# Hybrid S5 / HGRN2 block: three jobs side by side at the start, and S5 from step 12

## The chip, the cores and the metric

One core of a Trainium2 chip runs the whole program in one launch. The metric is the device time of one execution in microseconds (us), a median over runs; the profile is of one further execution. Engines in the profile: PE is TensorE (matmul), PEld its weight loads, DVE VectorE, ACT ScalarE, POOL GpSimd; SP issues most of the DMAs.

## The reference, cut to what matters

```python
h    = rmsnorm(x, ln_mix_g)                      # x: 256 tokens x 2048
proj = h @ w_in                                  # 2048 x 9216
u, q, f, i, g, gate_s5, gate_hgrn = split(proj)  # 5 x 1024, 2 x 2048
y_s5   = s5_branch(u) @ w_proj_s5                # complex scan, gelu, GLU with w_glu
y_hgrn = hgrn2_branch(q, f, i, g) @ w_proj_hgrn  # gated recurrence, chunked
merged = sigmoid(gate_s5) * y_s5 + sigmoid(gate_hgrn) * y_hgrn
x = x + merged @ w_out
x = x + conv_glu_ffn(rmsnorm(x, ln_ffn_g))       # w_up 2048 x 11264, w_down
out = rmsnorm(x, ln_final_g)
```

All in float32; the matmuls are made of split operands (below).

## The kernel before

**Steps and jobs.** Every large matrix is read once, in 480 steps of 512 KB. A step loads a piece of weights (load_step, line 247, tile wr, 4 buffers, queue of SP), splits it (split_step, line 252: ACT copies it into a rounded high part wh, then DVE subtracts for the low part wl, 3 buffers each) and multiplies it: 8 matmuls of wh with 512 columns (the high and low halves of the activations side by side) and 8 of wl with 256, or in the jobs written token by token 8 and 4 of 512. A job is some steps that add into one PSUM bank pair (tile mm, two of them) and an epilogue (`st.after`) that DVE and ACT run on the sum one step later. The jobs in order: 4 of u and 4 of q (4 steps each, steps 0 to 31), 2 of g (16 steps), 4 of f (16), 4 and 4 of the gates (64), 2 of v (16, up to step 143); then GLU (steps 144 to 151), w_proj_s5 (152 to 167), w_proj_hgrn (168 to 183), w_out, w_up and w_down.

**The start.** x is loaded in four chunks of 512 columns. x_chunk (line 393) transposes a chunk on PE in 8 transposes; ACT writes the high part of hT with the gain of the norm (line 405) and DVE the low part. x_first (line 419) does chunk 0 and the split of step 0, with 6 warm-up matmuls behind it (tile dummy, on ones); chunks 1 to 3 are put between the two halves of steps 0, 1 and 2 (`between`), so that a job takes one chunk per step. The 1/rms of the rows is not needed for the products: x_norm (line 427) squares x on DVE in 8 instructions, issued behind step 2, and broadcasts the result R_x with PE; epilogues multiply by it. x_params transposes packed parameters.

**The side work and its planner.** Two generators hold the work that is not of the weight steps: side_s5 (line 580; tables, then 8 tiles in two pairs each: projection b_proj on PE, two products on DVE, a scan on DVE, two products, an output on PE) and side_hgrn (line 874: loads of q, k, f, scores on PE and masks and products on DVE over 7 levels, then o, its norm, its transposes). side_run (line 1303) is called after each step from S5_START = 3 on and emits pieces of them while an account allows it: all instructions of DVE and PE are charged an estimate (lines 76 to 92), and a piece is emitted when DVE's sum isn't above PE's:

```python
rate = {"tensor_copy": 0.52, "tensor_scalar": 0.52, "reciprocal": 6.3}.get(name, 1.04)
return 0.065 + 1.12e-3 * rate * n
...
if force in done if force is not None else load["dve"] > load["pe"] + SIDE_LEAD:
    return
```

At most 2 (S5) or 3 (HGRN) pieces a step are emitted. HGRN comes when S5 is finished. Two due dates are hard: step 144 needs all of S5, and step 168 all of HGRN (`need`). What isn't emitted by then is emitted at once, in front of that step: `if st.need not in done: side_run(force=st.need)` (line 1350), whatever the account says.

**What orders the instructions.** The framework's scheduler takes the program's order as priorities: an engine's instructions are put into a fixed queue, and one of lower priority can be put ahead where the scheduler finds the engine free and its inputs and buffers ready. behind_x (line 414) forbids that for what is emitted within it: it stays behind the last chunk of x.

Of the kernel before, what the change touches and what calls it, by code (L numbers as in the profile page):

```python
# [10 lines left out]
F32 = mybir.dt.float32  # L11
F32R = mybir.dt.float32r
# [5 lines left out]
P = 128  # L18
D = 2048
T = 256  # L20
# [90 lines left out]
def kernel(  # L111
# [48 lines left out]
    def axbank():  # L160
        uid[0] += 1
        return psx.tile([P, 512], F32, tag="ax", name=f"ax{uid[0]}")

    def v3(t, n):
        return t.rearrange("p (a b) -> p a b", a=n)
# [8 lines left out]
            return self.units[k // 4][:, (k % 4) * T:(k % 4 + n) * T]  # L174


    ones = cst.tile([P, P], F32, name="ones")
    G.memset(ones, 1.0)
# [7 lines left out]
    S.dma_start(out=cf, in_=cst_f)  # L186
    ident = cf[:, C_ID:C_ID + P]

    x_tok = [[unit() for _ in range(2)] for _ in range(2)]
    pack = unit()  # L190
    packA, packB = pack[0:104, 0:P], pack[0:64, P:2 * P]
    packC = [pack[0:P if i < 2 else 96, (2 + i) * P:(3 + i) * P] for i in range(3)]
# [1 line left out]
    def rows(ap):  # L194
        return ap.rearrange("o (r c) -> (o r) c", c=P)

    packG = pack[0:16, 6 * P:7 * P]
    S.dma_start(out=packG, in_=rows(ln_mix_g))
    G.memset(packA, 0.0)
    ldt = pack[0:64, 5 * P:5 * P + 2]  # L200

# [38 lines left out]
    def weight_step(src, mm, need=None, extra_load=None):  # L240
        st = Step()
        st.src, st.mm, st.need, st.extra_load = src, mm, need, extra_load
        st.after = st.between = None
        steps.append(st)
        return st

    def load_step(st):
        uid[0] += 1
        st.w = wp.tile([P, 1024], F32, tag="wr", name=f"wr{uid[0]}", bufs=4)
        S.dma_start(out=v3(st.w, st.src.shape[1]), in_=st.src)  # L250

    def split_step(st):
        uid[0] += 1
# [17 lines left out]
    def fm_job(wap, c0, nkc, xs, epi, need=None, extra_load=None, wide=False):  # L271


        job = new_job()
        box = {}
        ng = nkc // 4
        for g in range(ng):
            def mm(st, g=g):
                if g == 0:
                    box["ps"] = mm_bank()  # L280
                ps = box["ps"]
                wh, wl = v3(st.wh, 4), v3(st.wl, 4)
                for part in range(2):
                    if part == 1 and st.between is not None:
                        st.between()
# [107 lines left out]
    def x_chunk(g, between=None):  # L393

        for h in range(2):
            if h == 1 and between is not None:
                between()
            ax = axbank()
            for a in range(2):
                for j in range(2):  # L400
                    c = (g % 2) * 512 + (2 * h + a) * P
                    lastp = PE.transpose(ax[:, a * T + j * P:a * T + (j + 1) * P], x_tok[j][g // 2][:, c:c + P], ident)
            for a in range(2):
                kc = 4 * g + 2 * h + a
                A.activation(out=hT[:, kc, 0, :], in_=ax[:, a * T:(a + 1) * T], func=AF.Copy, scale=g_mix[:, kc:kc + 1])  # L405
# [5 lines left out]
        box["x"] = [getattr(i, "ins", i) for i in (last, lastp)]  # L411

    @contextmanager
    def behind_x():

        with tc.issue_after(box["x"][0]), tc.issue_after(box["x"][1]):
            yield

    def x_first():
        ax = axbank()  # L420
        PE.transpose(ax[:, 0:16], packG, ident[:16, :16])
        V.tensor_copy(g_mix, ax[:, 0:16])
        x_chunk(0, lambda: split_step(steps[0]))
        with behind_x():
            warm_up(WARM_H, ones)

    def x_norm():
        ss = cst.tile([P, 2, 4], F32, name="ss_x")
        for g in range(4):
            for j in range(2):  # L430
                xc = x_tok[j][g // 2][:, (g % 2) * 512:(g % 2) * 512 + 512]
                junk = tmp()
                V.scalar_tensor_tensor(out=junk, in0=xc, scalar=1.0, in1=xc, op0=ALU.mult, op1=ALU.mult,
                                       accum_out=ss[:, j, g:g + 1])
# [3 lines left out]
        broadcast_rows(R_x, r_x)  # L438

    def x_params():  # L440
        ax = axbank()
# [89 lines left out]
    u_jobs = [fm_job(w_in, 256 * p, 16, xs_hw, epi_u(p), wide=True) for p in range(4)]  # L531
    for p in range(4):
        fm_job(w_in, 1024 + 256 * p, 16, xs_hw, epi_q(p), wide=True)
    for b in range(2):
# [339 lines left out]
    def side_hgrn():  # L874
        yield f_job
        mraw = reload_tile()
        S.dma_start(out=mraw[:, 0:112], in_=cst_m)
        V.tensor_copy(masks, v3(mraw[:, 0:80], 5))
        q, k, f = (Chunks(8) for _ in range(3))
        for p in range(4):  # L880
            for t, src in ((q, q_dram), (k, k_dram), (f, f_dram)):
# [443 lines left out]
                if pauses[0] >= PAUSES[side[0]]:  # L1325
                    return

    for i in range(LOAD_AHEAD):
        if i < 4:
            load_x_chunk(i)  # L1330
        load_step(steps[i])
        if i == 4:
            load_params()
    table_up()
    warm_up(WARM, ones)
    x_first()
    for i in range(1, LA):
        split_step(steps[i])
    for i in range(3):
        steps[i].between = lambda i=i: x_chunk(i + 1)  # L1340
    load["dve"] = load["pe"] = 0.0
    for i, st in enumerate(steps):
        if i + LOAD_AHEAD < len(steps):
            load_step(steps[i + LOAD_AHEAD])
        if i + LA < len(steps):
            split_step(steps[i + LA])
# [11 lines left out]
        if i == NORM_AT:  # L1358
            with behind_x():
                x_norm()  # L1360
                x_params()
        if st.after is not None:
            job, fn = st.after
            later.append((i + 1, job, fn))
        load["dve"] = max(load["dve"], load["pe"] - 4.0)
        if i >= S5_START:
            pauses[0] = 0
            if i == S5_START:
                with behind_x():
                    side_run()  # L1370
            else:
                side_run()
    run_later(i=len(steps) + 10)


# [28 lines left out]
```

## Time and profile before

| | |
|---|---|
| median of 3 runs | 1423.0 us (1422.8 to 1423.98) |
| the profiled execution | 1422.75 us, span 1420.6 us |
| PE busy | 1403.4 us (99% of the span) |
| DVE busy | 1056.9 us (74%) |
| ACT busy | 757.7 us (53%) |
| DMA | 278.58 MB, mean 196 GB/s |

A row of a timeline is: start, length (us), engine, line, operation, out<-in, shape, how many were merged, and in brackets how long the engine sat idle before it and what released it. The line is often 106, that of the helper which keeps the account; so tiles tell the work apart: mm is a weight step, ax a transpose or a small product, bu a projection of S5, u any of the large work tiles. A row of the chain of waits is start, length, what. A row of windows is the stretch, its length, then the busy time and count of PE, PEld, DVE, ACT and POOL, the granted clock of PE, the DMA share and GB/s.

### The profile page before, as it was taken

How to read it: one execution, taken by the hardware profiler on the slowest of the kernel's cores; microseconds unless marked ns; L12 is line 12 of the kernel's file. 1: busy time of each engine (PE TensorE's matmuls, PEld its weight loads, DVE VectorE, ACT ScalarE, POOL GpSimd, SP SyncE). 2: the span in 40 equal slices, each digit the busy share in tenths (PEclk: the TensorE clock that was granted, in tenths of full speed). 3: DMA queues.
4: the chain of work that ended last, by engine and by line, in shares of the span. 5: the costliest groups of instructions: out<-in, count | busy, mean ns of one | idle time of the engine just before them, and what ended most of it. 6: DMA issues, size and time to landing. Idle time of an engine off the chain costs nothing.

```text
span 1420.6 us, 20722 instructions
## 1 busy us (share of the span) xinstructions
PE 1403.4 (99%) x8008; PEld 1182.1 (83%) x8008; DVE 1056.9 (74%) x1453; ACT 757.7 (53%) x962; POOL 38.0 (3%) x33
## 2 busy tenths in 40 slices
PE   9999999999999999999999999999999999999997
PEld 7878887877778787888888888888888888888885
DVE  7999989998978968655777777777777775545454
ACT  5455576665655464454555555555555554434343
POOL 1040000000001000000000000000000000000000
PEclk9999999999999999999999999999999999999999
DMA  7865767666767466666666666666666666666653
GB/s 237 219 195 149 218 206 219 202 205 187 210 191 262 154 199 207 220 212 207 193 191 185 188 192 187 186 191 191 185 189 191 188 187 193 201 193 201 194 194 125
DMA packets 215940, 278.58 MB, mean 196 GB/s; under 512 B 19938, under 2 KB 141042, under 8 KB 215841
## 3 DMA queue, kind: packets, MB, share of 16 engines
q1 hardware_dynamic: 198496, 266.57, 60.5%
q10 hardware_dynamic: 17088, 10.49, 2.4%
q8 instruction: 63, 1.03, 0.3%
q14 instruction: 37, 0.30, 0.1%
q0 software_dynamic: 256, 0.19, 0.0%
HBM read 266.73 MB, written 10.49 MB: 195 GB/s over the span
## 4 chain that ended last, share of the span: by engine, by line
PE 95%; DVE 2%; DMA 1%; ACT 1%; issue 0%; POOL 0%; ACTq 0%; DVEq 0%; POOLq 0%
PE mm L106 87%; PE ax L106 7%; DVE u L106 1%; PE bu L106 1%; DMA u<-d 1%; DVE wl L106 1%; DMA u<-in_s_log_dt_dram 0%; ACT wh L256 0%; DVE t L106 0%; PE dummy L106 0%; DVE zmat L106 0%; ACT u L1275 0%; DVE x2g L106 0%; ACT hT L405 0%; ACT t L1259 0%
## 5 line engine op out<-in xcount | busy, mean ns | idle before, releaser
L256 ACT CAST wh<-wr 128x1024 fp32r<-128x1024 f32 x480 | 503.0, 1051 | 587.7 <-PE mm L106 424.2
L106 DVE TENSOR_TENSOR wl<-wr,wh 128x1024 fp32r<-128x1024 f32 x480 | 588.2, 1228 | 304.3 <-ACT wh L256 301.3
L106 PE MATMUL mm<-x2g,wh 128*128 128x512 f32 x1408 | 352.6, 392 | 0.0
L106 PEld LDWEIGHTS mm<-x2g,wh 128*128 128x128 f32 x1408 | 253.3, 189 | 45.3
L106 PE MATMUL mm<-wh,u 128*128 128x512 f32 x1040 | 260.7, 392 | 0.0
L106 PEld LDWEIGHTS mm<-wh,u 128*128 128x128 f32 x1040 | 193.7, 188 | 39.7
L106 PEld LDWEIGHTS mm<-x2g,wl 128*128 128x128 f32 x1408 | 192.0, 190 | 13.6
L106 PE MATMUL mm<-x2g,wl 128*128 128x256 f32 x1408 | 196.4, 282 | 0.0
L106 PE MATMUL mm<-wh,hT 128*128 128x512 f32 x768 | 193.6, 394 | 0.0
L106 PEld LDWEIGHTS mm<-wh,hT 128*128 128x128 f32 x768 | 142.1, 188 | 33.5 <-issue 2.9
L106 PE MATMUL mm<-wl,u 128*128 128x512 f32 x520 | 140.6, 390 | 0.0
L106 DVE TENSOR_TENSOR u<-u,u 128x512 f32<-128x512 f32 (+4 forms) x144 | 114.8, 821 | 0.5
L106 PEld LDWEIGHTS mm<-wl,u 128*128 128x128 f32 x520 | 97.4, 188 | 20.0
L106 PE MATMUL mm<-wl,hT 128*128 128x512 f32 x384 | 102.9, 390 | 0.0
L106 PE MATMUL mm<-hT,wh 128*128 128x512 f32 x384 | 100.4, 401 | 0.8 <-ACT wh L256 0.8
L106 PEld LDWEIGHTS mm<-wl,hT 128*128 128x128 f32 x384 | 72.1, 188 | 15.5
L106 PEld LDWEIGHTS mm<-hT,wh 128*128 128x128 f32 x384 | 69.9, 192 | 14.8 <-ACT wh L256 1.0
L106 DVE SCALAR_TENSOR_TENSOR t<-ub,colC,t 128x256 f32<-128x256 f32 x176 | 73.3, 479 | 0.0
L106 PEld LDWEIGHTS mm<-hT,wl 128*128 128x128 f32 x384 | 52.1, 191 | 4.7 <-DVE wl L106 1.3
L106 PE MATMUL mm<-hT,wl 128*128 128x256 f32 x384 | 54.3, 284 | 0.3 <-DVE wl L106 0.3
L1200 ACT ACTIVATE t<-ub,colC 128x256 f32<-128x256 f32 x88 | 48.0, 593 | 0.0
L106 PE MATMUL ax<-wh,u 128*128 128x512 f32 x176 | 43.3, 389 | 0.0
(186 smaller groups left out, 861.2 us busy)
## 6 DMA issues: line engine op xcount, KB each, us to landing
wr<-in_w_up_dram SPq DMA_DIRECT2D x176, 512.0 KB, 4.5
wr<-in_w_in_dram SPq DMA_DIRECT2D x144, 512.0 KB, 4.4
wr<-in_w_down_dram SPq DMA_DIRECT2D x88, 512.0 KB, 4.7
wr<-in_w_out_dram SPq DMA_DIRECT2D x32, 512.0 KB, 4.2
wr<-in_w_proj_s_dram SPq DMA_DIRECT2D x16, 512.0 KB, 4.0
wr<-in_w_proj_hgrn_dram SPq DMA_DIRECT2D x16, 512.0 KB, 4.8
d<-t ACTq DMA_DIRECT2D x28, 256.0 KB, 4.4
rl<-d SPq DMA_DIRECT2D x16, 256.0 KB, 4.3
```

The source lines that it names most:

```text
L106: return fn(*args, **kw)
L256: A.copy(st.wh, st.w)
L1200: A.activation(out=av, in_=ub[:, a, 0:T], func=AF.Identity, scale=conv_col(0, n), bias=colC[:, 264 + n:265 + n])
```

## The change

The first three jobs (12 steps) no longer run one after the other: their steps are taken chunk by chunk of x (`FRONT = 3`: step g of jobs 0, 1, 2, then step g + 1 of them), so that a chunk serves three steps. The third job has its own PSUM pair (front_bank). In these 12 steps the order on SP, PE, ACT and DVE is the one written (manual_schedule). The first chunk of x and the first weight tile come in halves, the weights and the constants from ACT's queue, and the first step (`fine`) multiplies half by half, 24 matmuls of 256 columns instead of 16. A split runs one step ahead there and not two; 3 warm-up matmuls for 6. The squares of x go to ACT, chunk by chunk. The planner's account is set to zero at step 12, and side_run is called from step 12 on.

```diff
-    WARM_H = 6
-    NORM_AT = 2
+    WARM_H = 3
+    FRONT = 3
...
+    def load_first():
+        st = steps[0]
...
+        for h in range(2):
+            for j in range(2):
+                S.dma_start(out=x_tok[j][0][:, h * T:(h + 1) * T], in_=x[0, j * P:(j + 1) * P, h * T:(h + 1) * T])
+            st.dma = A.dma_start(out=v3(st.w, 4)[:, 2 * h:2 * h + 2, :], in_=st.src[:, 2 * h:2 * h + 2, :])
...
+    def x_squares(g):
+        for j in range(2):
+            xc = x_tok[j][g // 2][:, (g % 2) * 512:(g % 2) * 512 + 512]
+            junk = tmp()
+            A.activation(out=junk, in_=xc, func=AF.Square, accum_out=ss_x[:, j, g:g + 1])
...
+    u_jobs = [fm_job(w_in, 256 * p, 16, xs_hw, epi_u(p), wide=True, bank=front_bank if p == 2 else mm_bank, fine=p == 0)
+              for p in range(4)]
+    steps[:4 * FRONT] = [steps[4 * p + g] for g in range(4) for p in range(FRONT)]
...
-    S5_START = 3
...
+    def load_front(i):
+        if i % FRONT == 0 and i < 4 * FRONT:
+            load_x_chunk(i // FRONT)
+        load_step(steps[i])
...
-            later.append((i + 1, job, fn))
+            later.append((i + (2 if i < 4 * FRONT else 1), job, fn))
+    ET = mybir.EngineType
+    with tc.manual_schedule(engines={ET.SP, ET.PE, ET.Activation, ET.DVE}):
+        load_first()
+        table_up()
+        for i in range(1, LOAD_AHEAD):
+            load_front(i)
+        warm_up(WARM, ones)
+        x_first()
+        for i in range(4 * FRONT):
+            g, r = divmod(i, FRONT)
+            load_front(i + LOAD_AHEAD)
+            if r == FRONT - 1 and g < 3:
+                x_chunk(g + 1)
+            split_step(steps[i + 1])
+            if i == 0:
+                x_squares(0)
+            elif r == FRONT - 1 and g < 3:
+                x_squares(g + 1)
+            work(i, steps[i])
+            if i == 3 * FRONT - 1:
+                x_norm()
+            elif i == 3 * FRONT + 1:
+                broadcast_rows(R_x, r_x)
+            elif i == 4 * FRONT - 1:
+                x_params()
+    for i in range(1, LA):
+        split_step(steps[4 * FRONT + i])
     load["dve"] = load["pe"] = 0.0
     for i, st in enumerate(steps):
+        if i < 4 * FRONT:
+            continue
...
         load["dve"] = max(load["dve"], load["pe"] - 4.0)
-        if i >= S5_START:
...
+        pauses[0] = 0
+        if i == 4 * FRONT:
+            with behind_x():
+                side_run()
+        else:
+            side_run()
```

x_first writes the same transposes, copies and splits for the two halves in turn, with the high part of the first 128 columns on DVE; then the 3 warm-up matmuls. The load of HGRN's masks is kept behind the last chunk of x and the load of step 12.

More of the change, by code (lines that the diff above doesn't have):

```diff
@@ L174, in at, with rows @@
             return self.units[k // 4][:, (k % 4) * T:(k % 4 + n) * T]
+    pack = unit()
+    packA, packB = pack[0:104, 0:P], pack[0:64, P:2 * P]
+    packC = [pack[0:P if i < 2 else 96, (2 + i) * P:(3 + i) * P] for i in range(3)]
+    def rows(ap):
+        return ap.rearrange("o (r c) -> (o r) c", c=P)
+    packG = pack[0:16, 6 * P:7 * P]
+    S.dma_start(out=packG, in_=rows(ln_mix_g))
     ones = cst.tile([P, P], F32, name="ones")
-    G.memset(ones, 1.0)
+    V.memset(ones, 1.0)
     epsc = cst.tile([P, 1], F32, name="epsc")
@@ L185 @@
     cf = cst.tile([P, C_N], F32, name="cf")
-    S.dma_start(out=cf, in_=cst_f)
+    A.dma_start(out=cf, in_=cst_f)
     ident = cf[:, C_ID:C_ID + P]
     x_tok = [[unit() for _ in range(2)] for _ in range(2)]
[L190 to L198, printed above, removed]
     G.memset(packA, 0.0)
@@ L242, in weight_step @@
         st.src, st.mm, st.need, st.extra_load = src, mm, need, extra_load
-        st.after = st.between = None
+        st.after = None
         steps.append(st)
@@ L249, in load_step @@
         st.w = wp.tile([P, 1024], F32, tag="wr", name=f"wr{uid[0]}", bufs=4)
[L250 removed]
+        st.dma = S.dma_start(out=v3(st.w, st.src.shape[1]), in_=st.src)
     def split_step(st):
@@ L279, in mm @@
                 if g == 0:
-                    box["ps"] = mm_bank()
+                    box["ps"] = bank()
                 ps = box["ps"]
                 wh, wl = v3(st.wh, 4), v3(st.wl, 4)
+                if fine and g == 0:
+                    for h, part in ((0, 0), (0, 1), (0, 2), (1, 0), (1, 1), (1, 2)):
+                        for k in (2 * h, 2 * h + 1):
+                            for j in range(2):
+                                cols = slice(j * P, (j + 1) * P)
+                                o = ps[:, j, T:] if part == 1 else ps[:, j, :T]
+                                PE.matmul(o, (wl if part == 2 else wh)[:, k, cols], hT[:, k, part % 2, :],
+                                          start=k == 0 and part == 0, stop=False)
+                    return
                 for part in range(2):
-                    if part == 1 and st.between is not None:
-                        st.between()
                     for j in range(2):
@@ L391, in load_x_chunk, with x_chunk @@
                         in_=x[0, j * P:(j + 1) * P, g * 512:(g + 1) * 512])
-    def x_chunk(g, between=None):
+    def load_first():
+        st = steps[0]
+        uid[0] += 1
+        st.w = wp.tile([P, 1024], F32, tag="wr", name=f"wr{uid[0]}", bufs=4)
         for h in range(2):
-            if h == 1 and between is not None:
-                between()
+            for j in range(2):
+                S.dma_start(out=x_tok[j][0][:, h * T:(h + 1) * T], in_=x[0, j * P:(j + 1) * P, h * T:(h + 1) * T])
+            st.dma = A.dma_start(out=v3(st.w, 4)[:, 2 * h:2 * h + 2, :], in_=st.src[:, 2 * h:2 * h + 2, :])
+    def x_chunk(g):
+        for h in range(2):
             ax = axbank()
@@ L410, in x_chunk @@
                                               op0=ALU.mult, op1=ALU.subtract)
-        box["x"] = [getattr(i, "ins", i) for i in (last, lastp)]
+        box["x"] = [getattr(i, "ins", i) for i in (last, lastp, lasta)]
     @contextmanager
     def behind_x():
-        with tc.issue_after(box["x"][0]), tc.issue_after(box["x"][1]):
+        with tc.issue_after(box["x"][0]), tc.issue_after(box["x"][1]), tc.issue_after(box["x"][2]):
             yield
     def x_first():
+        st = steps[0]
+        uid[0] += 1
+        st.wh = wp.tile([P, 1024], F32R, tag="wh", name=f"wh{uid[0]}", bufs=LA + 1)
+        st.wl = wp.tile([P, 1024], F32R, tag="wl", name=f"wl{uid[0]}", bufs=LA + 1)
         ax = axbank()
@@ L422, in x_first @@
         V.tensor_copy(g_mix, ax[:, 0:16])
-        x_chunk(0, lambda: split_step(steps[0]))
-        with behind_x():
-            warm_up(WARM_H, ones)
-    def x_norm():
[L428 to L434, printed above, removed]
+        for h in range(2):
+            ax = axbank()
+            half = slice(h * 512, h * 512 + 512)
+            A.copy(st.wh[:, half], st.w[:, half])
+            for a in range(2):
+                for j in range(2):
+                    c = (2 * h + a) * P
+                    PE.transpose(ax[:, a * T + j * P:a * T + (j + 1) * P], x_tok[j][0][:, c:c + P], ident)
+            for a in range(2):
+                kc = 2 * h + a
+                xa, gk = ax[:, a * T:(a + 1) * T], g_mix[:, kc:kc + 1]
+                if kc == 0:
+                    V.tensor_scalar(out=hT[:, kc, 0, :], in0=xa, scalar1=gk, scalar2=None, op0=ALU.mult)
+                else:
+                    A.activation(out=hT[:, kc, 0, :], in_=xa, func=AF.Copy, scale=gk)
+            for a in range(2):
+                kc = 2 * h + a
+                V.scalar_tensor_tensor(out=hT[:, kc, 1, :], in0=ax[:, a * T:(a + 1) * T], scalar=g_mix[:, kc:kc + 1],
+                                       in1=hT[:, kc, 0, :].bitcast(F32), op0=ALU.mult, op1=ALU.subtract)
+            V.tensor_tensor(out=st.wl[:, half], in0=st.w[:, half], in1=st.wh[:, half].bitcast(F32), op=ALU.subtract)
+        warm_up(WARM_H, ones)
+    ss_x = cst.tile([P, 2, 4], F32, name="ss_x")
+    def x_squares(g):
+        for j in range(2):
+            xc = x_tok[j][g // 2][:, (g % 2) * 512:(g % 2) * 512 + 512]
+            junk = tmp()
+            A.activation(out=junk, in_=xc, func=AF.Square, accum_out=ss_x[:, j, g:g + 1])
+    def x_norm():
+        ss = ss_x
         ssum = cst.tile([P, 2], F32, name="ssum_x")
@@ L529, with front_bank @@
     gh_dram = [[scratch() for _ in range(2)] for _ in range(4)]
-    u_jobs = [fm_job(w_in, 256 * p, 16, xs_hw, epi_u(p), wide=True) for p in range(4)]
+    def front_bank():
+        uid[0] += 1
+        return psb.tile([P, 2, 512], F32, tag="bu", name=f"mf{uid[0]}")
+    u_jobs = [fm_job(w_in, 256 * p, 16, xs_hw, epi_u(p), wide=True, bank=front_bank if p == 2 else mm_bank, fine=p == 0)
+              for p in range(4)]
+    steps[:4 * FRONT] = [steps[4 * p + g] for g in range(4) for p in range(FRONT)]
     for p in range(4):
@@ L876, in side_hgrn @@
         mraw = reload_tile()
-        S.dma_start(out=mraw[:, 0:112], in_=cst_m)
-        V.tensor_copy(masks, v3(mraw[:, 0:80], 5))
+        with behind_x(), tc.issue_after(getattr(steps[4 * FRONT].dma, "ins", steps[4 * FRONT].dma)):
+            S.dma_start(out=mraw[:, 0:112], in_=cst_m)
+            V.tensor_copy(masks, v3(mraw[:, 0:80], 5))
         q, k, f = (Chunks(8) for _ in range(3))
@@ L1326, in side_run, with work @@
                     return
-    for i in range(LOAD_AHEAD):
-        if i < 4:
-            load_x_chunk(i)
+    def load_front(i):
+        if i % FRONT == 0 and i < 4 * FRONT:
+            load_x_chunk(i // FRONT)
         load_step(steps[i])
[L1332 to L1346, printed above, removed]
+        if i == 3 * FRONT + 1:
+            with tc.issue_after(getattr(steps[i].dma, "ins", steps[i].dma)):
+                load_params()
+    def work(i, st):
         run_later(i=i)
@@ L1357 @@
         st.mm(st)
[L1358 to L1361, printed above, removed]
         if st.after is not None:
             job, fn = st.after
-            later.append((i + 1, job, fn))
-        load["dve"] = max(load["dve"], load["pe"] - 4.0)
-        if i >= S5_START:
[L1367 to L1371, printed above, removed]
+            later.append((i + (2 if i < 4 * FRONT else 1), job, fn))
[26 more added lines that the diff above has]
+        split_step(steps[4 * FRONT + i])
+    load["dve"] = load["pe"] = 0.0
+    for i, st in enumerate(steps):
+        if i < 4 * FRONT:
+            continue
+        if i + LOAD_AHEAD < len(steps):
+            load_front(i + LOAD_AHEAD)
+        if i + LA < len(steps):
+            split_step(steps[i + LA])
+        work(i, st)
+        load["dve"] = max(load["dve"], load["pe"] - 4.0)
+        pauses[0] = 0
+        if i == 4 * FRONT:
+            with behind_x():
                 side_run()
+        else:
+            side_run()
     run_later(i=len(steps) + 10)
```

6 lines of the change are left out of this document (3 added, 3 removed).

## The prediction

> **What bounds the kernel now.** I read the page's first two parts, then PE's waits, the timeline from 0 to 70 us and around 100, 450 and 540 us, and windows there.
>
> ```profile
> PE 1403.4 (99%) x8008; PEld 1182.1 (83%) x8008; DVE 1056.9 (74%) x1453; ACT 757.7 (53%) x962; POOL 38.0 (3%) x33
> ...
> PE   9999999999999999999999999999999999999997
> ...
> DVE  7999989998978968655777777777777775545454
> ```
>
> PE is never free except at the ends, so time can come only from a later or earlier first product, from stalls, or from work that PE loses or gains; the change takes no product away. DVE is at nine tenths while the side work runs (to slice 16, some 570 us), and far below that after it. The rows of a plain step:
>
> ```profile
> 49.97 2.00 PE L106 MATMUL mm<-hT,wh 128*128 128x512 f32 x8
> ...
> 52.77 2.00 PE L106 MATMUL mm<-hT,wh 128*128 128x512 f32 x8
> ```
>
> One step to the next is 2.80 us. Steps 11 and 12 are the rows at 47.07 (below) and 49.97, counted from the first product.
>
> **Part 1, the start.**
>
> ```profile
> 6.92 1.54 PE ax L106 x6
> ...
> 20.98 0.55 PE ax L106 x5
> ...
> 36.19 0.60 PE ax L106 x5
> ...
> 37.40 0.20 PE ax L106
> ...
> 38.03 0.32 PE ax L106 x3
> ```
> ```profile
> 7.86 1.57 ACT L405 ACTIVATE hT<-ax,g_mix 128x256 fp32r<-128x256 f32 x4 [5.62 <-PE ax L106]
> ...
> 8.26 2.43 PE L106 MATMUL dummy<-ones 128*128 128x128 f32 x12
> 9.31 1.06 ACT L256 CAST wh<-wr 128x1024 fp32r<-128x1024 f32 x1
> ...
> 10.56 2.08 PE L106 MATMUL mm<-hT,wh 128*128 128x512 f32 x8
> ...
> 47.07 2.12 PE L106 MATMUL mm<-hT,wh 128*128 128x512 f32 x8 [0.78 <-ACT wh L256]
> ```
> ```profile
> 6.00:7.00 1.00, 0.70 (x3) 0.26 (x3) 0.32 (x2) 0.00 (x0) 0.20 (x4) 1.00 0.99 312
> 7.00:8.00 1.00, 1.00 (x5) 1.00 (x6) 0.00 (x0) 0.14 (x1) 0.00 (x0) 1.00 1.09 391
> ```
>
> Before, the first product (10.56) waits for the cast of step 0, which ACT runs behind four evictions of x. From there to step 12 are 39.4 us; 12 steps are 33.6, 24 transposes at 0.11 (the row at 20.98) 2.6, R_x and its like 0.6. Another 0.5 goes to the first transposes of S5 (37.40 and 38.03), which only move. 2.1 us are lost, 0.78 of them in the row at 47.07.
>
> After, x, whose chunk is there now when the six transposes start at 6.92, has the constants off its queue and comes half by half; 312 to 391 GB/s flow at that time, so the 0.5 MB of the weight tile, on the other queue, is at most 1.5 us apart from it. I take 7.0 for the second half of both. Half of the evictions and of the cast are done by then. What stands behind the second half: 4 transposes at 0.11 to 0.26 (row at 6.92: 1.54 for 6), 0.4 to 1.0 us, then 3 warm-ups, half of the 2.43 us: the first product at about 8.8 (8.2 to 9.6), 1.8 us earlier. In the 12 steps then, by in-order queues: ACT per three steps has three casts (1.06), four evictions (0.4 each) and two squares (as a 512-wide pass on ACT, bounded by 0.5 and 1.1 from half of and the whole cast), 6 to 7 us; DVE less; PE has 9.3 us in them. So neither binds, the splits keep up at a lead of one step, and of the 2.1 us lost I leave 0.3 for the 8 extra weight loads. But there is less warm-up: the transposes at 6.92 take 0.26 us where later ones take 0.11, so PE ran at half pace until the dummies had lasted, and step 0, begun 1.8 us sooner, may run part of its 2.8 us at that pace: 1.0 (0 to 2). Sum of part 1: 1.8 + 1.8 - 1.0 = 2.6 us gained (1 to 4.5).
>
> On the last term the Trainium skill (TensorE: Matmul & The Clock Gate, Part 1) says that the clock stays at half until some 3.4 us of sustained activity, which speaks against cutting the warm-up. By that rule, counted from the second half's transposes at 7.0, 1.6 us of step 0 would run at half pace, 0.8 be lost, and 2.8 gained instead of 2.6.
>
> **Part 2, the tables of S5 (steps 22 to 30 now).**
>
> ```profile
> 77.83 11.68 POOL L741 TENSOR_TENSOR u<-u 128x1024 f32<-128x1024 f32 x3 [71.63 <-DVE u L106]
> ...
> 83.48 4.25 DVE L106 TENSOR_SCALAR u<-u,cf 128x512 f32<-128x512 f32 x2
> ...
> 100.48 0.87 DVE L106 TENSOR_SCALAR u<-u,cf 128x512 f32<-128x512 f32 x2
> ...
> 101.50 1.14 PE L106 MATMUL ax<-cf,u 128*128 128x128 f32 x8 [2.33 <-DVE u L106]
> ...
> 102.32 3.67 PE L106 MATMUL mm<-hT,wh 128*128 128x512 f32 x8
> ```
> ```profile
> 104.00:106.00 2.00, 2.00 (x7) 1.56 (x7) 0.60 (x1) 1.37 (x2) 0.00 (x0) 0.56 0.80 202
> ```
>
> DVE is late here: two instructions that take 0.87 at 100 us take 4.25 beside POOL's additions. PE waits 2.33 us for it, its granted clock falls to 0.56, and the next eight products take 3.67 instead of 2.00: 4.0 us gone. After the change DVE comes to this stage without the squares, and with its splits done; but the same instructions meet the same work of POOL. Gain between 0 and 4.0, or a loss of up to 2.3, one such wait more, if the pieces fall closer together; I take 2.0, between none and all of it, since no row is nearer to either.
>
> **Part 3, the due dates.** Here the change costs. I added up the planner's charges over the program's order. A plain step gives PE 2.62 (8 x 0.218 + 8 x 0.109) and DVE 1.26 for the low part, so the account of S5 grows by 1.36 a step, less 1.32 for an epilogue. Before, chunks and squares put it at -3.6 behind step 2; -2.2, -2.2, -0.8 and +0.5 follow, so the first piece is emitted behind step 6. Pieces and credit then stay in balance, and the last one falls behind step 143: one step ahead of its due date. After, the account is zero at step 12, where the first piece goes out. That is 6 steps of credit less, 6 x 1.36 = 8.2 (8.3 by the full sum): some 8 us of DVE's work, from a scan to the last split, is left at step 144 and is emitted at once. PE's part of S5 can't drift ahead, since products of higher priority are always ready: the projections lie in the trace where they are emitted. What this costs is read from the end of S5 now:
>
> ```profile
> 413.89 0.97 PE L106 MATMUL bu<-u 32*128 32x256 f32 x12
> ...
> 427.37 2.35 DVE L106 TENSOR_TENSOR u<-bu,u 128x1024 f32<-128x1024 f32 x2
> ...
> 433.11 2.42 DVE L106 TENSOR_TENSOR_SCAN u<-mag,u 128x256 f32<-128x256 f32 x4
> ...
> 436.57 2.48 DVE L106 TENSOR_TENSOR u<-u,u 128x1024 f32<-128x1024 f32 x2
> ...
> 440.10 1.29 DVE L106 TENSOR_TENSOR u<-u,u 128x512 f32<-128x512 f32 x2
> ...
> 444.98 1.07 PE L106 MATMUL ax<-u,u 128*32 128x256 f32 x16
> ...
> 450.42 1.29 DVE L106 TENSOR_TENSOR u<-u,u 128x512 fp32r<-128x512 f32 x2
> ...
> 451.64 2.23 PE L106 MATMUL mm<-u,wh 128*128 128x512 f32 x9
> ```
> ```profile
> L106 DVE TENSOR_TENSOR wl<-wr,wh 128x1024 fp32r<-128x1024 f32 x480 | 588.2, 1228 | 304.3 <-ACT wh L256 301.3
> ```
>
> The last projection (413.89, behind step 131) goes to the last split (450.42 + 1.29 = 451.7), and step 145, the first that needs it, starts at 451.6: no slack at all. The chain from output to split took 6.7 us; in front of it stand 2.35 + 2.42 + 2.48, two sums of 1.3 each, and six splits of 1.2 between them, so 24 us at the least from the projection. After, the projection comes behind step 138, and step 145 is only 6 steps and an output, 17.9 us, away: 6 us of PE's time if DVE never waits, and up to 12 if the first products only start behind step 143, as their place in the order says (now they start 13 us after the projection). I take 6, the lower, because the row is a schedule with other work between, and steps of another job can fill 2.8 us.
>
> The second due date is worse, because the forced pieces are charged too. The account stands at -10 in front of step 144 and climbs by 1.36 a step, less 2.0 for each epilogue of GLU: it is positive again behind step 157. So HGRN is emitted from 157 and not from 144, with its due date, 168, unmoved.
>
> ```profile
> 459.51 0.64 PE L106 MATMUL ax<-u,ones 128*32 128x256 f32 x8
> ...
> 512.27 1.29 DVE L106 TENSOR_TENSOR u<-u,u 128x512 f32<-128x512 f32 x2
> ...
> 540.18 1.08 PE L106 MATMUL mm<-wh,u 128*128 128x512 f32 x4
> ```
> ```profile
> 460.00:480.00 20.00, 18.52 (x407) 15.03 (x404) 19.82 (x29) 9.74 (x15) 1.82 (x1) 1.00 0.48 156
> 480.00:500.00 20.00, 20.00 (x390) 15.61 (x390) 19.79 (x37) 9.07 (x13) 0.00 (x0) 1.00 0.60 193
> ```
>
> HGRN's first product lies in step 147 (459.51; its loads came late), step 168 starts at 540.18: 80.7 us with 20.6 steps, 57 us, so some 21 us of PE's own for HGRN and 3 of waiting. Up to 513.6 DVE is full (19.8 of 20), 54 us; without the splits and epilogues of the steps that will no longer lie there, about 43. Then come 26.6 us of o, norm and transposes, of which PE could do without some 6. After, from 157.5 to 168 PE has 10.5 steps, 29 us, and its 21: 50 us, for a chain of 43 + 20 = 63 at best and 43 + 26.6 at worst. PE waits 13 to 20 us, less what DVE's free time from step 145 on lets it do ahead. I take 13.
>
> **Sum.** Against the profiled execution, 1422.75: -2.6 - 2.0 + 6 + 13 = +14.4, so 1437.2; the median of the runs lies 0.25 above that execution, so 1437.4. Everything behind step 168 is as before and moves with it.
>
> **The rivals.**
>
> ```profile
> 33.96 0.18 DVE L106 CAST masks<-rl 128x80 uint8<-128x80 f32 x1
> ```
> ```profile
> 400.00:420.00 20.00, 20.00 (x108) 15.55 (x107) 16.18 (x19) 9.17 (x10) 0.96 (x1) 1.00 0.67 207
> 420.00:440.00 20.00, 20.00 (x90) 16.58 (x89) 16.19 (x17) 9.30 (x10) 0.00 (x0) 1.00 0.63 184
> ```
>
> (1) Faster: both due dates are met, because the scheduler puts the side work into DVE's free time and DVE's real times are below the charges. For it: DVE is busy for 16.2 of 20 us between 400 and 440 us, and the masks of HGRN, emitted at step 144, were made at 33.96, so free time is used; it decides when the last projection is at most 24 us ahead of step 145 by PE's order. Against it: PE's pieces are bound to their place. The time is 1423.0 - 4.6 = 1418.4 (1415 to 1420). (2) Only S5 is late, and HGRN, whose pieces are ready once the loads are in, is drawn into PE's waiting: 1418.4 + 6 = 1424.4 (1421 to 1430). (3) The start has stalls of its own: splits at a lead of one step, with the chunk of x in the same queues ahead of them, make PE wait in each third step. The bound is an ACT with 7 us per 9.3, so this decides only if the loads of w come more than 2 us late; then 4 waits of 1 to 3 us, 1 + 8 on top of either.
>
> **How the numbers follow.** About 0.2% (2.8 us) is what a measurement of this kernel can tell from no change. The forecast has 0.55, (1) 0.22, (2) 0.18 (half within 0.2%, the rest shared, a little more to slower), (3) alone 0.05. So faster 0.25, the same 0.09, slower 0.66. The forecast's own range is 1428 (S5 at its least, half of the wait for HGRN) to 1447 (both at their most, part 2 at nothing). To leave out no more than 2 in 10 the range reaches down to the middle of (1), 1418.
>
> **What would show it.** Right: the first product at 8.2 to 9.6 us; step 12 near 47; the tables of S5 six steps later; PE waits with DVE busy on u tiles at the start of GLU, about 145 steps in; DVE well below full for some 30 us behind that; a second, longer wait of PE, with a low granted clock behind it, in front of the products of w_proj_hgrn. Wrong: PE without waits over 2 us between 420 and 560 us, or HGRN's first product within five steps of GLU's first.

## The result, and the profile after

| | median | runs | ratio to before |
|---|---|---|---|
| before | 1423.29 us | 4 (1422.8 to 1423.98) | |
| after | 1446.33 us | 4 (1443.22 to 1447.27) | 1.0159 (1.0143 to 1.0174) |

The change costs 23 us. The profiled execution of after is its shortest (1443.22, span 1441.2), so the two traces differ by 20.6 us of span (1441.2 - 1420.6), 2.4 less than the medians (23.0).

The page of after (a slice is 36 us). PE, at 9 in every slice but the last before, has 8 in the fifteenth and sixteenth (504 to 576 us), and its clock in the sixteenth:

```profile
PE 1407.5 (98%) x8010; PEld 1184.1 (82%) x8010; DVE 1054.3 (73%) x1440; ACT 762.1 (53%) x978; POOL 31.4 (2%) x32
...
PE   9999999999999988999999999999999999999997
...
DVE  5898989999987695756677777777777775545454
...
PEclk9999999999999998999999999999999999999999
```

DVE starts at 5 and 8 where it had 7 and 9, and has 6 from 468 to 504 us, in the fourteenth slice, where it had 9. To date the loss I follow four places: the first product, step 12, step 144 (the first of GLU) and step 168. PE's timeline of after:

```profile
8.09 1.20 PE L106 MATMUL mm<-hT,wh 128*128 128x256 f32 x8
...
11.05 2.00 PE L106 MATMUL mm<-hT,wh 128*128 128x512 f32 x8
...
44.88 2.09 PE L106 MATMUL mm<-hT,wh 128*128 128x512 f32 x8
...
446.02 2.11 PE L106 MATMUL mm<-u,wh 128*128 128x512 f32 x8
...
450.52 0.64 PE L106 MATMUL ax<-u,u 128*32 128x256 f32 x8 [1.44 <-DVE u L106]
...
452.07 3.20 PE L106 MATMUL mm<-u,wh 128*128 128x512 f32 x7
...
458.43 3.50 PE L106 MATMUL mm<-u,wh 128*128 128x512 f32 x8 [1.98 <-DVE u L106]
...
463.03 1.99 PE L106 MATMUL mm<-u,wh 128*128 128x512 f32 x8
...
503.62 0.64 PE L106 MATMUL ax<-u,ones 128*32 128x256 f32 x8 [1.64 <-POOL u L948]
...
540.08 11.24 PE L106 MATMUL ax<-u,u 128*64 128x64 f32 x96 [2.87 <-DVE u L106]
...
557.55 1.96 PE L106 MATMUL ax<-cf,u 128*128 128x128 f32 x7 [6.24 <-DVE u L106]
559.35 0.79 PE L106 MATMUL mm<-wh,u 128*128 128x512 f32 x1
```

and the two rows of before that answer to 446.02 and 463.03 (steps 144 and 147):

```profile
448.87 1.98 PE L106 MATMUL mm<-u,wh 128*128 128x512 f32 x8
...
457.23 2.00 PE L106 MATMUL mm<-u,wh 128*128 128x512 f32 x8
```

| stretch | before | after | difference |
|---|---|---|---|
| start to step 12 | 49.97 | 44.88 | -5.1 |
| step 12 to 144 | 398.9 | 401.1 | +2.2 |
| step 144 to 147 | 8.4 | 17.0 | +8.6 |
| step 147 to 168 | 82.9 | 96.3 | +13.4 |
| step 168 to the end of the span | 880.4 | 881.9 | +1.4 |

So the start gains 5 us, and 22 are lost between steps 144 and 168. PE's waits from 430 to 570 us, after and then before:

```profile
PE ax L106 <- DVE u L106: 10.7, 4, 6.2
PE ax L106 <- POOL u L948: 2.1, 2, 1.6
PE mm L106 <- DVE u L106: 2.0, 1, 2.0
PE ax L106 <- issue: 1.6, 2, 1.2
```

```profile
PE ax L106 <- DVE u L106: 1.0, 1, 1.0
PE ax L106 <- issue: 0.5, 1, 0.5
```

The waits alone are 15 us more. Part of the rest is what follows a wait: the granted clock (the number behind POOL's) falls behind the waits at the start of GLU and behind those between 540 and 558 us, though not behind the waits for GpSimd near 504 us. Windows of after:

```profile
440.00:460.00 20.00, 16.59 (x77) 12.01 (x76) 15.06 (x19) 9.03 (x11) 1.90 (x2) 0.89 0.49 145
460.00:480.00 20.00, 19.68 (x104) 17.03 (x103) 13.21 (x16) 14.06 (x21) 0.00 (x0) 0.94 0.44 144
480.00:500.00 20.00, 20.00 (x89) 16.54 (x89) 11.79 (x13) 9.38 (x11) 0.00 (x0) 1.00 0.76 239
500.00:520.00 20.00, 16.00 (x380) 11.41 (x379) 18.35 (x28) 3.32 (x4) 4.88 (x2) 1.00 0.79 264
...
540.00:560.00 20.00, 13.56 (x105) 12.42 (x106) 7.86 (x25) 11.47 (x44) 0.00 (x0) 0.78 0.28 93
```

DVE, busy for 19.8 of 20 us between 460 and 500 us before, now stands idle for 7 and 8 of each 20 there: no work of HGRN is in its queue yet. Its first product comes at 503.62, 44 us later than before (459.51), and its end then decides when step 168 may start. The chain of waits of after, in front of that step, goes from 547 us on through ACT and small steps of DVE, and comes back to PE only with the transposes:

```profile
551.94 2.34 ACT t L1048 x16
...
557.55 1.96 PE ax L106 x7
```

### The profile page after: what moved, and what is told of

It is laid out like the page before. It is cut to its first block, busy times and chain, and to the rows that moved or that the text cites. A ratio compares the mean times of both kernels' runs of the same rounds, so it can differ in the third digit from the quotient of the medians.

```text
span 1441.2 us, 20729 instructions
## 1 busy us (share of the span) xinstructions
PE 1407.5 (98%) x8010; PEld 1184.1 (82%) x8010; DVE 1054.3 (73%) x1440; ACT 762.1 (53%) x978; POOL 31.4 (2%) x32
## 4 chain that ended last, share of the span: by engine, by line
PE 65%; DVE 1%; ACT 1%; DMA 1%; issue 0%; DVEq 0%; SPq 0%
PE mm L106 59%; PE ax L106 6%; DVE u L106 1%; DMA u<-d 0%; DMA wr<-in_w_proj_s_dram 0%; ACT t L1048 0%; DVE wl L106 0%; ACT wh L256 0%; ACT u L1044 0%; ACT u L1322 0%; ACT L358 0%; DVE x2g L106 0%; DVE rss L106 0%; ACT u L1018 0%; ACT t L1306 0%
## 5 line engine op out<-in xcount | busy, mean ns | idle before, releaser
L106 DVE TENSOR_TENSOR wl<-wr,wh 128x1024 fp32r<-128x1024 f32 (+1 forms) x481 | 589.9, 1230 | 308.9 <-ACT wh L256 301.1
L106 DVE TENSOR_TENSOR u<-u,u 128x512 f32<-128x512 f32 (+4 forms) x144 | 110.7, 796 | 2.7 <-DMA rl<-in_cst_m_dram 1.6
L106 PE MATMUL mm<-hT,wh 128*128 128x512 f32 (+1 forms) x360 | 89.1, 389 | 1.6 <-ACT wh L256 1.6
L106 PEld LDWEIGHTS mm<-hT,wh 128*128 128x128 f32 x360 | 63.9, 189 | 13.7 <-ACT wh L256 1.8
L106 PEld LDWEIGHTS mm<-hT,wl 128*128 128x128 f32 x352 | 47.8, 190 | 6.2 <-DVE wl L106 3.0
L106 PE MATMUL mm<-hT,wl 128*128 128x256 f32 x352 | 49.5, 283 | 1.9 <-DVE wl L106 1.9
```

The lines of the kernel that those rows point to most:

```text
L106: return fn(*args, **kw)
```

## The experiments

The theory: both losses behind step 144 come from the planner's account, which reaches step 144 with 8.3 us of S5's work not emitted, and step 157 before HGRN is emitted. The rivals: the new start itself makes S5 late, or DVE's time is short everywhere, so that no credit helps.

**The late account with the old start.** The kernel before, with only this edit:

```diff
-    S5_START = 3
+    S5_START = 12
+        if i == S5_START:
+            load["dve"] = load["pe"] = 0.0
```

> The kernel before with its own start, S5 from step 12 and the account set to zero there. By the charges 8.3 us of S5 are left at step 144, HGRN starts at step 155 and 10.2 us of DVE's and 10.2 us of PE's part are left at step 168, nearly as in the changed kernel (8.3; step 157; 11.6 and 10.8). Theory: the same two waits, 20 us on top of the kernel before, 1439 to 1446 us. Rival (the new start is the cause): 1421 to 1426 us.

Measured: 1441.33 us (1438.65 to 1441.79), 1.0121 (1.0104 to 1.0137). PE's waits from 430 to 580 us are those of after: 9.8 us for DVE in three, 2.7 for POOL, 2.1 for a u tile of GLU, 1.7 for issue. The first product of HGRN comes at 492.3 us. So 18 of the 23 us need nothing of the new start. What is left, 5.0 us (1446.33 - 1441.33), is a loss by the new start, though its step 12 comes sooner.

**Only the six steps, the account kept.** As above without the reset.

> The kernel before with S5 from step 12 on, its account left as it is: the credit that gathers from step 6 to step 12 is kept up to the ceiling of 4 us. By the charges only 3.0 us are left at step 144 and 3.9 us at step 168. Theory (what counts is the credit, not the step at which S5 begins): 1 to 8 us above the kernel before, 1424 to 1431 us, well under the kernel with the account at zero. Rival (the late begin itself costs): within 3 us of that one, about 1440 us.

Measured: 1432.27 us (1431.78 to 1433.12), 1.0061 (1.0046 to 1.0076): half of the 18 us, and 1.3 us above the upper end of what was expected. What I had not counted fits the waits in the stage of the tables, where the pieces now fall closer together: one of 3.7 us near 105 us (before has 2.3 near 101) and one of 1.1 for wl. Near 545 us PE waits for 4.3.

**The credit given back at once at step 12.** The changed kernel with

```diff
     load["dve"] = load["pe"] = 0.0
+    load["pe"] = 8.2
...
-        load["dve"] = max(load["dve"], load["pe"] - 4.0)
+        load["dve"] = max(load["dve"], load["pe"] - 8.2)
```

> The changed kernel with the planner's account started at 8.2 us in PE's favour at step 12 instead of zero (and its ceiling at 8.2 instead of 4): the same start, the same steps, only the side work is emitted as early, in steps before its due dates, as it was before the change. Adding up the charges, nothing is left at step 144 and HGRN is emitted from step 144 to 166. Theory (the account's six lost steps cause the loss): the waits of PE near 450 us and between 500 and 560 us are gone, 22 us less, so 1419 to 1425 us. Rival (the loss comes from the new order at the start or from the buffers that the side work finds): the waits stay, 1436 us or more.

Measured: 1434.29 us (1432.89 to 1434.96), 1.0074 (1.0059 to 1.0089): neither. The waits behind 430 us went (1.3 for DVE and 0.9 for issue are left), and others came at 60 to 120 us. Its window there, and its first wait from 60 to 430 us:

```profile
60.00:80.00 20.00, 14.50 (x78) 12.51 (x77) 19.15 (x91) 7.84 (x10) 0.00 (x0) 0.93 0.67 209
```

```profile
PE mm L106 <- DVE t L106: 5.5, 1, 5.5
```

DVE is full there with 91 instructions, and PE waits 5.5 us for an epilogue that stands behind them. So credit at the stage of the tables buys a wait there: the rival is right for that stage.

**The forced pieces not charged.** The changed kernel with, behind the forced emission at step 144,

```diff
+                if st.need == "s5":
+                    load["dve"] = min(load["dve"], load["pe"])
```

> The changed kernel, with the charge of the forced S5 pieces forgiven at step 144 (DVE's sum is set down to PE's there). By the charges 8.3 us of S5 are still forced at step 144, but HGRN is emitted from 144 to 167 and nothing is forced at 168. Theory of two separate waits: the wait near 450 us stays (about 8 us), the one between 500 and 560 us goes (about 14 us), so 1430 to 1434 us. Rival (HGRN is late because S5's data are late, whatever the account): the second wait stays, 1440 us or more.

Measured: 1429.39 us (1428.59 to 1430.68), 1.0042 (1.0028 to 1.0056). HGRN's first product comes at 466.60 us, and from 480 to 580 us PE waits for nothing, while the waits at the start of GLU are still there (1.4 and 2.1 us). So the second, larger loss is the charge for the forced pieces, and the first is what is emitted too late. Not all of the 17 us that came back (1446.33 - 1429.39) are that charge. In the two profiles steps 144 to 147 take 14.0 us instead of 17.0, with nearly the same waits (1.4 and 2.0 in after) but at a granted clock of 1.00 (windows from 448 to 472 us), and nothing in the edit sets that pace; behind step 147 the time is 13.3 us shorter.

**The credit given late and spread.** The changed kernel with

```diff
         load["dve"] = max(load["dve"], load["pe"] - 4.0)
+        if 80 <= i < 140:
+            load["pe"] += 0.18
```

> The changed kernel, but PE's account gets 0.18 more behind each of steps 80 to 139, 10.8 in all: the 8.3 that the reset at step 12 took, given back late and spread, behind the stage of S5's tables. Theory (the dates are missed by the planner's charges, and DVE has free time between 300 and 440 us, where it was busy 16.2 of 20): S5 is finished by step 144, HGRN is emitted from there, both waits of PE over 2 us behind 430 us go, and nothing is added at 80 to 110 us: 1418 to 1424. Rival (DVE's time is short everywhere, so that what is emitted sooner makes PE wait sooner, as the credit at step 12 did): the waits show up between 250 and 440 us instead, 1429 or more.

Measured: 1424.53 us (1422.85 to 1426.38), 1.0009 (1.0000 to 1.0019). Both waits are gone: between 250 and 580 us none is over 0.7 us. DVE, busy for 72.7 of 80 us between 360 and 440 us in after, is busy for 79.2 here, so it had the time. That is 22 us back (1446.33 - 1424.53), by a credit of 10.8 us where the reset had taken 8.3; but the 5 us of the earlier step 12 do not show in the time.

**S5's tables on GpSimd's queue.** In the changed kernel the four loads of these tables are issued by ACT. The timelines of ACT and PE of after around it, and that of ACT in the kernel with the old start and the late account:

```profile
45.47 5.16 ACTq L631 DMA_DIRECT2D u<-in_s_b_im_dram  x1
...
50.65 3.31 ACTq L633 DMA_DIRECT2D u<-in_s_c_re_dram  x1
...
54.72 2.95 ACT L256 CAST wh<-wr 128x1024 fp32r<-128x1024 f32 x3 [9.08 <-PE mm L106]
...
55.81 2.11 PE L106 MATMUL mm<-hT,wh 128*128 128x512 f32 x8 [1.62 <-ACT wh L256]
```

```profile
50.89 3.48 ACTq L585 DMA_DIRECT2D u<-in_s_b_im_dram  x1
54.40 3.55 ACTq L587 DMA_DIRECT2D u<-in_s_c_re_dram  x1
...
58.70 2.96 ACT L256 CAST wh<-wr 128x1024 fp32r<-128x1024 f32 x3 [7.25 <-DVE u L106]
```

Both issues hold ACT, and three casts come late in one go. With the old start PE doesn't wait for them; with the new one it waits 1.62 us. The edit, on the kernel with the forgiven charge:

```diff
-            A.dma_start(out=v3(dst, 32), ...
+            G.dma_start(out=v3(dst, 32), ...
...
-            A.dma_start(out=v3(dst, 8), ...
+            G.dma_start(out=v3(dst, 8), ...
```

> The kernel of the forgiven account (the forced pieces of S5 not charged, 1429.4), with the four loads of S5's tables issued by GpSimd and not by ScalarE. In the changed kernel they hold ScalarE for 5.2 and 3.3 us each at 45 to 54 us, and its casts stand behind them. Theory A (that hold is what steps 12 to 30 lose): PE's waits on casts and on wl near 45 to 60 us go, 1 to 3 us, 1426 to 1428. Theory B (the loss in the table stage is that of VectorE beside GpSimd's additions, at 90 to 105 us): within 0.7 us of 1429.4, and the waits there unchanged.

Measured: 1429.14 us (1428.48 to 1430.85), as without it. But this tells neither theory apart, for the loads went elsewhere: GpSimd isn't bound to the written order, issued them at 6 to 11 us, beside the chunks of x; PE's wait near 56 us is gone, and it waited near 21 us instead:

```profile
21.04 2.14 PE L106 MATMUL mm<-hT,wh 128*128 128x512 f32 x8 [2.36 <-ACT wh L256]
```

The same with the spread credit:

> The changed kernel with both edits: the credit of 10.8 spread over steps 80 to 139, and the four table loads on GpSimd's queue. If the credit and the loads each bring what their theories say and lie in different stages, the two add: 1416 to 1422, faster than the kernel before. If the loads are covered anyway: the same as with the credit alone. If VectorE's time is short everywhere: 1429 or more.

Measured: 1423.65 us (1422.51 to 1425.89), 1.0003 (0.9994 to 1.0012), with waits at the front again (2.2 for a cast, and 1.4 for a later chunk of x). A third run was to keep the loads behind the load of step 12, by the same call as the masks of HGRN:

> The changed kernel with the credit of 10.8 spread over steps 80 to 139, and the four loads of S5's tables on GpSimd's queue, this time kept behind the load of step 12. In the two runs before, GpSimd issued them at 6 to 11 us, beside the chunks of x, and PE waited 2.2 to 2.4 us on a cast near 21 us, 1.4 more on x in one of them. Theory A (the hold of ScalarE at 45 to 54 us costs 1.6 to 1.9 us, and the early loads cost about as much): both waits go, 1420 to 1423. Theory B (what PE gains there VectorE takes back in the table stage behind it): 1423.5 to 1425, as with the credit alone.

Measured: 1425.04 us (1423.34 to 1425.66), 1.0010 (1.0001 to 1.0019). The edit did not do what it says: GpSimd's timeline has the first of these loads at 6.13 us again, so its expectation was not put to the test. What the loads cost on GpSimd's queue at their proper place stays open.

**No warm-up.** The changed kernel with `WARM_H = 0`.

> The changed kernel with no warm-up matmuls behind the first transposes (0 for 3). Step 0 took 2.96 us there, at full pace. Theory of the prediction's last term (the clock needs the sustained work of the dummies): step 0 starts up to 1 us sooner but runs part of its length at half pace, its 24 matmuls taking 4 us or more, and step 12 does not come sooner than 44.9 us. Rival (the pace is full by then from the transposes and the earlier dummies): the first product comes at 7.2 to 7.6 us, takes 3 us again, and step 12 comes about 0.5 us sooner, at 44.3.

Measured: 1444.21 us in one run. PE's timeline, and a row of DVE's:

```profile
7.66 1.62 PE L106 MATMUL mm<-hT,wh 128*128 128x256 f32 x8
...
9.37 0.74 PE L106 MATMUL mm<-hT,wl 128*128 128x256 f32 x4
...
11.38 2.00 PE L106 MATMUL mm<-hT,wh 128*128 128x512 f32 x8
```

```profile
8.64 0.68 DVE L106 TENSOR_TENSOR wl<-wr,wh 128x512 fp32r<-128x512 f32 x1
```

Between the two: the product comes 0.43 us sooner, step 0 takes 3.72 us instead of 2.96 (11.05 - 8.09), and step 12 comes at 45.21, not sooner. The first eight products take 1.62 us where after's take 1.20. That does not show that the clock needs the dummies: the granted clock is 1.00 in the windows from 7.66 to 12 us, and the low half of the weight tile leaves DVE only at 9.32 (8.64 + 0.68), just in front of PE's products with it at 9.37. In after it leaves DVE at 8.47, in front of its products at 9.13. So step 0 there fits a wait for DVE. Nor is 3.72 us out of the way: in the eight profiles with three dummies and this first step it takes 2.96 to 4.26. Longest is the kernel with the forgiven charge:

```profile
8.32 2.05 PE L106 MATMUL mm<-hT,wh 128*128 128x256 f32 x8
```

Its granted clock is 0.50 from 8 to 10 us, with the three dummies and x there as early as in after (first product at 8.32). Three dummies were enough in after's profile and not in that one.

**The old start with the spread credit.** The kernel before with S5 from step 12, the account reset, and the two lines of the spread credit.

> The kernel before, its own start untouched, with S5 from step 12 on, the account set to zero there, and the credit of 10.8 spread over steps 80 to 139. Without the credit it took 1441.3, 5 us less than the changed kernel, although its step 12 came 3.5 us later: between steps 12 and 144 it had 1.3 us of waits, the changed kernel 4.9. Theory A (the new start gives back what it gains, since it hands over splits with a lead of one and work of VectorE undone): 1418 to 1421, below the changed kernel with the same credit (1424.5) and below the kernel before. Theory B (with the dates met the new start keeps its 3 us): 1426 or more.

Measured: 1419.53 us (1418.59 to 1420.35), 0.9973 (0.9962 to 0.9983): faster than both kernels. Its waits from 60 to 580 us:

```profile
PE ax L106 <- DVE u L106: 2.0, 3, 1.3
PE mm L106 <- DVE wl L106: 0.8, 1, 0.8
...
```

With this the two questions stand in one square (medians, us):

| | old start | new start | difference |
|---|---|---|---|
| account zero at step 12 | 1441.33 | 1446.33 | +5.0 |
| and the credit spread over steps 80 to 139 | 1419.53 | 1424.53 | +5.0 |
| difference | -21.8 | -21.8 | |

The spread credit is worth 21.8 us with either start, and the new start costs 5.0 with either account. Of the 21.8, the reset and the late step had taken 18.0 from the old start (1441.33 - 1423.29); the other 3.8 are a gain that before does not have. About half of them fits the stage of the tables, where before loses 4.0 us (2.33 of waiting, 1.67 in slow products) and this kernel waits for 2.1 with the granted clock at 1.00.

**A lead of two splits.** Why does the new start lose, though its step 12 is 1.7 us earlier (46.86 against 48.56 in the profiles of the second row)? DVE's column (the third) in the windows of after, then of the kernel with the old start and the late account, from 20 to 60 us:

```profile
20.00:40.00 20.00, 20.00 (x122) 17.77 (x122) 12.73 (x24) 12.50 (x25) 0.00 (x0) 1.00 0.68 209
40.00:60.00 20.00, 18.38 (x107) 15.93 (x106) 16.02 (x50) 8.14 (x11) 0.00 (x0) 1.00 0.91 211
```

```profile
20.00:40.00 20.00, 20.00 (x120) 17.44 (x119) 19.06 (x44) 10.21 (x15) 0.00 (x0) 1.00 0.60 188
40.00:60.00 20.00, 20.00 (x117) 17.44 (x116) 13.73 (x61) 6.31 (x8) 0.00 (x0) 1.00 0.87 198
```

DVE does 4.0 us less there, but that is not work left for later: the eight squares of x, 4.9 us of DVE with the old start, went to ACT. What the new start hands over undone is one split step more, for it has one ahead and not two, and epilogues: all three of the first jobs lie between 43.7 and 50.7 us, around and behind step 12, where the old start has one of them left. The kernel with the spread credit, and this:

```diff
-            split_step(steps[i + 1])
+            for s in ([i + 1] if i < 5 else [6, 7] if i == 5 else [i + 2]):
+                split_step(steps[s])
...
-    for i in range(1, LA):
+    for i in range(2, LA):
```

> The changed kernel with the credit of 10.8 spread over steps 80 to 139, and from step 5 on in the first 12 steps the splits run two steps ahead instead of one, so that step 12 is reached with two split steps in hand, as elsewhere. Theory A (the new start gives its gain back because it hands over a lead of one: PE waits 1.6 to 2 us on a cast near 56 us, behind the hold of ScalarE by the loads of S5's tables, and 2 us on wl near 195 us): the wait at 56 us goes, and the time is 1421 to 1422.5. Theory B (VectorE's work that was left undone in the first 12 steps is what makes PE wait, near 100, 120, 195 and 220 us): the wait at 56 us may go but others take its place, 1424 to 1425.5.

Measured: 1422.21 us (1420.2 to 1423.22), 0.9990 (0.9981 to 0.9999), 2.3 us below the same kernel with a lead of one; the runs of the two overlap only between 1422.85 and 1423.22. PE's rows:

```profile
56.35 2.11 PE L106 MATMUL mm<-hT,wh 128*128 128x512 f32 x8 [0.43 <-ACT wh L256]
...
194.66 1.21 PE L106 MATMUL mm<-hT,wl 128*128 128x256 f32 x8 [1.17 <-DVE wl L106]
```

The wait near 56 us fell from 1.94 to 0.43 us, and the one near 195 us, for a split of DVE, stayed (1.4 with a lead of one). So of the 5 us the lead is about half. The other 2.7 stay open. This kernel still waits for DVE near 117, 195 and 220 us (2.4 us together), but the old start with the same credit waits for it near 103 and 117 us too (2.1): between steps 12 and 144 all waits are 3.6 us here and 2.1 there, some 1.5 more, and I took none of them away.

## Why the prediction was right, and where it was not

**Direction and cause: right.** The loss is at the two due dates, in the order forecast, and not at the start. The signs it named for the dates are there: PE waits at the start of GLU with DVE on u tiles, DVE well below full for 30 us and more behind that, a longer wait with a low clock in front of w_proj_hgrn. Those for the start and the tables are a little off: the first product at 8.09 (8.2 to 9.6 was named), step 12 at 44.88 (near 47), and the tables seven steps later instead of six (the transposes that waited in step 29 wait in step 36). The experiments on the account show the cause and not only the place: the losses come with the old start too, the second goes when the forced pieces aren't charged, both go when the credit is given back.

**The sum: too small.** The forecast was +14.4 against the profiled execution, the profiles give +20.5; the median of 1446.33 lies 8.9 above the forecast of 1437.4 and close to the upper end of the range, 1447. Term by term:

| term | forecast | in the profiles | from |
|---|---|---|---|
| start | -2.6 | -4.6 | -5.1, less the 0.5 that only moved |
| step 12 to 144 | -2.0 | +2.6 | +2.2, less that 0.5, and 0.9 for 12 products of S5's outputs that now lie behind 144 |
| S5 at step 144 | +6 | +7.7 | +8.6, less that 0.9 |
| HGRN at step 168 | +13 | +14.8 | 13.4, and 1.4 behind it |

The errors do not all point one way: the start gained 2.0 us more than forecast and so hid part of what the other three terms cost more (4.6, 1.7 and 1.8). The median of after lies another 2.9 us off (1446.33 - 1443.22 = 3.1 here, 0.25 forecast). In the profiles of four other kernels with this same start step 12 comes at 46.0 to 46.9 us, and in the profiled one at 44.88, so its start was a lucky one; that the other three runs of after began like those four is not shown, for they have no trace.

*Start.* The first product came 2.5 us sooner and not 1.8, and 2.1 us of lost time were regained, 1.8 forecast. The term of 1.0 (0 to 2) for part of step 0 at half pace came to nothing in this profile, where step 0 took 2.96 us; in the seven other profiles with three dummies step 0 took 0 to 1.3 us longer, the 1.3 at a granted clock of 0.50, so the term can be paid, inside its range, and this execution escaped it. A bound of the working was a little low: at 312 GB/s the 0.5 MB of the weight tile take 1.7 us and not 1.5, but the sum does not use it. The Trainium skill (TensorE: Matmul & The Clock Gate, Part 1) would have 3.4 us of sustained work before the full pace; work alone does not settle it here, for after ran at full pace from 8.09 and the kernel with the forgiven charge, with the same work ahead of it, had a granted clock of 0.50 from 8 to 10 us.

*Tables.* This term had the wrong sign. I let DVE come to that stage "without the squares, and with its splits done". It comes with one split in hand and with three epilogues behind step 12; and ACT's hold, which a lead of two covers, costs a wait. DVE's split beside GpSimd's additions takes 2.96 us where others take 1.2, but that is so with the old start too (2.95 in the kernel with the spread credit). The rows of after:

```profile
92.86 6.53 POOL L787 TENSOR_TENSOR u<-u 128x1024 f32<-128x1024 f32 x3 [86.72 <-DVE u L106]
...
97.51 2.96 DVE L106 TENSOR_TENSOR wl<-wr,wh 128x1024 fp32r<-128x1024 f32 x1
...
100.53 1.22 PE L106 MATMUL mm<-hT,wl 128*128 128x256 f32 x8 [0.70 <-DVE wl L106]
...
117.27 1.07 PE L106 MATMUL ax<-cf,u 128*128 128x128 f32 x8 [0.71 <-DVE u L106]
```

The wait of 2.33 us, now the row at 117.27, shrank to 0.71, and the 1.7 us of slow products behind it are gone; but PE now waits in five more places between steps 12 and 144, 4.9 us in all where before had 2.6. That makes 0.6 of the term's +2.6; the other 2.0 lie in many rows that take a little longer, and I have no cause for them.

*S5.* Forecast 6, at the lower end of 6 to 12, measured 7.7. The account's six steps were right. Two waits (1.44 and 1.98) and the slow products behind each (3.20 for 7, 3.50 for 8) make up the cost; the pace was left out. It is not always paid: with the forgiven charge the same waits were followed by products at full pace, and these steps cost 5.6 us more than before and not 8.6.

*HGRN.* Forecast 13, measured 14.8. Its first product lies at 503.62, in step 160 and not in step 147, where the working had the first piece behind step 157: the loads, issued with that piece, take the rest, and PE's wait there is for GpSimd's work on them. The 1.4 us behind step 168 fit its slow first products: the granted clock is 0.73 in the 4 us from 559.35 on.

**The rivals.** The first (both dates met) is out: 15 us of waits. The second (HGRN drawn into PE's waiting) is out: its pieces are bound to where they are emitted; with the charge forgiven, which is what it needed, the time was 1429.4. The third (stalls of the start) was not in the first 12 steps, but the new start does cost 5 us, behind them; the rival had the place wrong, and its 4 waits are not what the cost is made of.

## What to carry to other kernels

Where a planner gives out side work by an account, a reset or a later start moves every later due date: add the account up to each date, and look at what forced work does to it, for the charge for 8 us of late work cost about twice what the late work did (14.8 against 7.7 in the profiles). A credit of 10.8 us was worth 22 us spread where DVE had time, and one of 8.2 was worth 12 us where DVE was full, so ask of each stage which engine has the time. Judge a new start some steps behind it: here the first product came 2.5 us sooner and the kernel 5 us later, about half of it because one split less was handed over; the cause of the other half stays open. And read a row of the first microseconds in several profiles: one of them had step 0 at 2.96 us, another at 4.26.

## What the runs showed of the hardware

- A short wait of PE can cost more than its length, and does not always. In after a wait of 1.98 us at 456 us was followed by eight products in 3.50 us instead of 2.0; in the kernel with the forgiven charge the same products behind a wait of 2.11 us took 2.24. A window of after, and the row of the other kernel:

```profile
458.00:462.00 4.00, 3.57 (x10) 2.71 (x11) 0.97 (x2) 0.04 (x1) 0.00 (x0) 0.64 0.45 135
```

```profile
459.06 2.24 PE L106 MATMUL mm<-u,wh 128*128 128x512 f32 x8 [2.11 <-DVE u L106]
```

The granted clock is 0.64 behind the one wait and 1.00 behind the other.

- One DMA issue of 256 KB on ACT's queue held ACT for 3.3 to 5.2 us, where the one before it took 0.38 and the last of the four 0.60; issued by GpSimd the four took 0.9 to 1.7 us each.
- GpSimd's additions stretched a split of DVE with two inputs from 1.2 to 2.96 us. The Trainium skill (GPSIMD Engine Reference, 1. Specifications) says that GpSimd shares its SBUF interfaces with VectorE and that instructions with two SBUF inputs contend; the row agrees with that.
- In kernels whose first steps are the same the first product came between 8.09 and 9.65 us. PE waited for x for 0.6 to 1.3 us in all ahead of it, and the three dummies took 0.83 us in one profile and 1.49 in others. Those 1.6 us are about as much as the 1.8 that the new start was to bring there.
